# Output projection in order of tokens, and two products of the MLP's first pair set ahead of the last tile's turn

## The chip, the cores and the metric

The kernel runs on one core of a Trainium2 chip. The metric is the device time of one execution in microseconds (us). The trace is of one profiled execution on the chip; all times in it count from the start of its span.

## The reference, cut to what matters

Two layers of a hybrid encoder work on 512 prompt tokens and 256 sample tokens, all in 32-bit floats. What the change touches is the end of the mixer and the start of the MLP:

```python
def encoder_layer(x, ...):
    ...                                     # three branches, gated and summed: merged
    x = x + merged @ w_out                  # output projection, 1024 x 1024
    h2 = rmsnorm(x, norm_ffn)
    u = dwconv(h2 @ ffn_w_up, ffn_conv_w, ffn_conv_b)   # 1024 x 5632
    val, gt = jnp.split(u, 2, axis=-1)
    return x + (jax.nn.silu(gt) * val) @ ffn_w_down
```

## The kernel before

**Tiles and splits.** The 768 tokens are six tiles of 128: tiles 0 to 2 are the first half of the tokens, tiles 3 to 5 the second (`TH` is 384). Each 32-bit operand is split into a high part (an ACT copy to fp32r) and a low part (a DVE subtraction), and each product is three matmuls: high x high, low x high, high x low. Activations are held turned (features on the partitions) in `hTh` and `hTl`.

**The up-projection by pairs.** `pair_products` computes two blocks of 128 features for all tokens by a scheme of seven half-size products instead of eight. With the inputs cut into two halves of the features and two halves of the tokens (`R["11"]`, `R["21"]` for the first half of the tokens, `R["12"]`, `R["22"]` for the second), it needs the sums t1 = 12 - 11, t2 = 22 - t1, t3n = 11 - t2 and t4n = 21 - t2. t1 stands in the place of `R["12"]` in `hTh`/`hTl`; t2, t3n and t4n are the tensors `Eh`/`El`. One product is 12 matmuls of 384 columns.

**What happens to one tile.** In the output projection `t_mm` does 24 matmuls of 512 columns for one tile and one half of the features (line 1265, `wo`); line 1266 adds the result to `x`. In the second half of the features each tile is then normalised (`norm_rows`: a square with sum on ACT, two small operations on POOL, a scaling on DVE, line 427, tile `xn`) and one step later turned (`quad`: eight transposes on TensorE, line 330, tile `tp`). This text calls those transposes the tile's turn.

- A tile of the first half (0 to 2) needs little of DVE afterwards: two low parts (`put`, line 435, `hTl<-tp`). Its turned halves are kept in `qt`.
- A tile of the second half (3 to 5) needs much: t1 (line 461), the low part of 22, t2 (line 464), the low part of t1 (`hTl<-qt`), and then in `e_sums` the low part of t2, two subtractions (lines 469 and 471) and the low parts of t3n and t4n (`El`): nine operations of 128x512.

**The order around the change.** `ORDER` is (0, 3, 1, 4, 2, 5): the tiles of the two halves alternate. The MLP begins with `up(0)`, whose `pair_products` gets `first`: the last tile is turned when `todo[0]()` is evaluated, ahead of the first product X = 11 x w11, and what `quad` returned, `e_sums` of the last tile, runs behind X. The order in which each engine takes its instructions is made by the framework's scheduler, from the order of the code and from its own estimates; `soon` raises an instruction's priority. Each engine works through its own list in order.

**Weights.** `Weights` brings them from memory (`wraw`), splits them on ACT (`whi`, line 206) and DVE (`wlo`, line 207) into six slots, and forms the sums that the pairs need (DVE, lines 217 and 229). A pair takes four slots; the output projection's half takes four too.

Of the kernel before, what the change touches and what calls it, by code (L numbers as in the profile page):

```python
# [9 lines left out]
AF = mybir.ActivationFunctionType  # L10
OP = mybir.AluOpType
# [8 lines left out]
NT = T // P  # L20
# [263 lines left out]
def body(tc, nc, a, depth=DEPTH):  # L284
# [8 lines left out]
    act, tt, stt, ts = (nc.scalar.activation, nc.vector.tensor_tensor,  # L293
                        nc.vector.scalar_tensor_tensor, nc.vector.tensor_scalar)
# [4 lines left out]
    def mxbank(name, tag=None):  # L299

        if tag is None:
            turn[0] ^= 1
            tag = ("mx", "my")[turn[0]]
        return psum.tile([P, 512], F32, name=name, tag=tag, bufs=BANKS[tag])
# [24 lines left out]
    def tr(out, in_):  # L329
# [8 lines left out]
    lo_, hi_ = slice(0, TH), slice(TH, T)  # L338

    R = {"11": [h[:, 0:4, lo_] for h in hT], "21": [h[:, 4:8, lo_] for h in hT],  # L340
         "12": [h[:, 0:4, hi_] for h in hT], "22": [h[:, 4:8, hi_] for h in hT]}
# [28 lines left out]
    def acc_tile():  # L370

        return {0: mxbank("acc", "acc"), TP: mxbank("acc", "acc")}
# [10 lines left out]
    def t_mm(o, t, ws, n, kper):  # L383
        ts_ = slice(t * P, (t + 1) * P)
        for k in range(NK):
            wh, wl = ws[k // kper]
            cs = slice((k % kper) * n, (k % kper) * n + n)
            mm(o, hT[0][:, k, ts_], wh[:, cs], start=(k == 0), stop=False)  # L388
            mm(o, hT[0][:, k, ts_], wl[:, cs], start=False, stop=False)  # L389
            mm(o, hT[1][:, k, ts_], wh[:, cs], start=False, stop=(k == NK - 1))  # L390
# [18 lines left out]
    def st4(name):  # L409
        return base.tile([P, 1024], F32, name=name, tag="st4", bufs=2)  # L410
# [27 lines left out]
    ORDER = (0, 3, 1, 4, 2, 5)  # L438
# [43 lines left out]
    def norm_then(step, t, x, gb, *args):  # L482

        xn = st4("xn")
        norm_rows(xn, x, gb)
        return lambda: step(t, xn, *args)


    def prod(bank, w, r, first):
        for k in range(4):  # L490
            o = bank[:, :TH]
            mm(o, w[0][:, k, :], r[0][:, k, :], start=first and k == 0, stop=False, skip_group_check=True)  # L492
            mm(o, w[0][:, k, :], r[1][:, k, :], start=False, stop=False, skip_group_check=True)  # L493
            mm(o, w[1][:, k, :], r[0][:, k, :], start=False, stop=k == 3, skip_group_check=True)  # L494

    def soon(ins, *args, **kw):
        with tc.high_priority(offset=100):
            ins(*args, **kw)  # L498

    def pair_products(v, g, tmp, done, vtag="acc", pump=0.0, first=None):  # L500

        wa, wb, wd, wc = W.get(4)
        cut = lambda w, o: tuple(x[:, o:o + 512].rearrange("p (k c) -> p k c", c=P) for x in w)
        w = {"11": cut(wa, 0), "22": cut(wa, 512), "12": cut(wd, 0),
             "s2": cut(wb, 0), "s1": cut(wb, 512), "s3": cut(wc, 0), "s4n": cut(wc, 512)}
        p1, u = tmp[:, :TH], tmp[:, TH:T]
        acc = lambda tag="acc": mxbank("acc", tag)[:, :TH]
        X = acc()  # L510
        prod(X, w["11"], R["11"], True)
        soon(act, p1, X, AF.Copy)
        if first:

            first()
            Z = acc()
            prod(Z, w["s1"], R["t1"], True)
            soon(act, g[:, lo_], Z, AF.Copy)
            prod(X, w["12"], R["21"], False)
            soon(act, v[:, lo_], X, AF.Copy)  # L520
            prod(Z, w["s4n"], R["22"], False)
            Y = acc()
            prod(Y, w["s2"], R["t2"], True)
            soon(tt, u, Y, p1, op=OP.subtract)
            soon(stt, v[:, hi_], Z, -1.0, u, op0=OP.mult, op1=OP.subtract)
            V = acc(vtag)
            prod(V, w["22"], R["t4n"], True)
            prod(Y, w["s3"], R["t3n"], False)
            soon(tt, u, Y, p1, op=OP.subtract)
            soon(tt, g[:, hi_], g[:, lo_], u, op=OP.add)  # L530
            soon(tt, g[:, lo_], V, u, op=OP.add)
            W.free(4)
            done(1)
            done(0)
            return
        side.pump(pump)
        pending()
        Y = acc()
        prod(Y, w["s2"], R["t2"], True)
        soon(tt, u, Y, p1, op=OP.subtract)  # L540
        side.pump(pump)
        prod(X, w["12"], R["21"], False)
        soon(act, v[:, lo_], X, AF.Copy)
        W.free()
        side.pump(pump)
        V = acc(vtag)
        prod(V, w["22"], R["t4n"], True)
        W.free()
        side.pump(pump)
        prod(Y, w["s3"], R["t3n"], False)  # L550
        soon(tt, g[:, hi_], Y, p1, op=OP.subtract)
        soon(tt, g[:, lo_], V, g[:, hi_], op=OP.add)
        side.pump(pump)
        Z = acc()
        prod(Z, w["s1"], R["t1"], True)
        soon(tt, g[:, hi_], Z, g[:, hi_], op=OP.add)
        W.free()
        side.pump(pump)
        done(1)

        def rest():
            prod(Z, w["s4n"], R["22"], False)
            soon(stt, v[:, hi_], Z, -1.0, u, op0=OP.mult, op1=OP.subtract)
            W.free()
            side.pump(pump)
            done(0)

        late.append(rest)
# [3 lines left out]
    def pending():  # L572
        while late:
            late.pop(0)()

    def load_gb(i):
        gb = base.tile([P, D], F32, name="gb", tag="gb", bufs=1)
        nc.sync.dma_start(gb, a["norms"][i])
        return gb
# [8 lines left out]
    def layer(l, x_in, prev_x):  # L588
# [559 lines left out]
        def pair(pool, tag, bufs, pump, evac):  # L1148
            vg = [pool.tile([P, T], F32, name=n, tag=tag, bufs=bufs) for n in ("pv", "pg")]
            tmp = pool.tile([P, T], F32, name="pt", tag=tag, bufs=bufs)  # L1150
            pair_products(*vg, tmp, lambda j: evac(j, vg[j]), pump=pump)
# [70 lines left out]
        for b in range(3):  # L1222
# [4 lines left out]
            for mp in range(4):  # L1227
                (wh, wl), = W.get()
                v = lambda w: w[:, :D].rearrange("p (m k c) -> p m k c", m=2, c=P)
                for mi in range(2):  # L1230
# [3 lines left out]
                    acc = acc_tile()  # L1234
# [18 lines left out]
        def ftile(name, tag, bufs=1, dt=F32):  # L1253
            return (ap if tag in ("ah", "al") else fp).tile([P, T], dt, name=name, tag=tag, bufs=bufs)
# [4 lines left out]
        todo = []  # L1259
        for half in range(2):  # L1260
            ws = W.get(4)
            cs = slice(half * 512, half * 512 + 512)
            for t in ORDER:
                ps = mxbank("wo")
                t_mm(ps, t, ws, 512, 2)
                tt(x[:, t, cs], x[:, t, cs], ps, op=OP.add)
                if half == 1:
                    bs = [f() for f in todo]
                    todo = [norm_then(quad, t, x[:, t, :], gb2,
                                      lambda i: ftile("qt", ("ah", "al", "rv", "uv")[i], (4, 4, 1, 1)[i]))]  # L1270
                    for f in bs:
                        f()


        def up(i):

            raw = [ftile("rv", "rv"), ftile("rg", "rg")]
            us = {}
            out = [ftile("ah", "ah", 4, F32R), ftile("al", "al", 4, F32R)]

            def conv(s):
                r, u = raw[s], ftile("u", ("uv", "ug")[s])
                f = i + NFF * s
                w = lambda j: par[:, O_FW + f * 3 + j:O_FW + f * 3 + j + 1]
                act(u, r, AF.Identity, scale=w(1), bias=par[:, O_FB + f:O_FB + f + 1])
                for c0, n in RANGES:
                    stt(u[:, c0 + 1:c0 + n], r[:, c0:c0 + n - 1], w(0), u[:, c0 + 1:c0 + n],
                        op0=OP.mult, op1=OP.add)
                    stt(u[:, c0:c0 + n - 1], r[:, c0 + 1:c0 + n], w(2), u[:, c0:c0 + n - 1],
                        op0=OP.mult, op1=OP.add)  # L1290
                us[s] = u
                if s == 1:
                    act(u, u, AF.Silu)
                    return
                ah, al = out
                tt(u, u, us[1], op=OP.mult)
                act(ah, u, AF.Copy)
                tt(al, u, ah.bitcast(F32), op=OP.subtract)

            pair_products(*raw, st4("pt"), conv, "po", first=todo[0]() if i == 0 else None)  # L1300
            return out

        fin = {}
# [21 lines left out]
        for gi, g in enumerate(DOWN_GROUPS):  # L1325
# [24 lines left out]
            for i, (t, cs) in enumerate(units):  # L1350
# [12 lines left out]
                if end and not last:  # L1363
                    nc.sync.dma_start(x_scr[tsl], x[:, t, :])
                    if i == 1:
                        gbn, todo = load_gb(2 * l + 2), []
# [3 lines left out]
                    todo = [norm_then(spill, t, x[:, t, :], gbn, stage, f_scrs[l + 1], "my")]  # L1370
# [29 lines left out]
```

## Time and profile before

| | |
|---|---|
| time, median of 3 runs | 2605.66 us (2602.86 to 2612.2) |
| the profiled execution's own time | 2605.65 us |
| its span in the trace | 2603.9 us |
| TensorE (PE) busy | 2560.1 us, 98% |
| VectorE (DVE) busy | 1904.2 us, 73% |
| ScalarE (ACT) busy | 1153.4 us, 44% |

Busy is the share of the span in which an engine had an instruction under way; matmuls overlap, so a busy PE is not one at its peak. PE rows are matmuls, PEld rows their weight loads.

### The profile page before, as it was taken

To read this page: it belongs to the slowest core of one execution; us is meant where nothing else is said; L and a number is where in the kernel's file an instruction comes from. 1 tells how busy PE (TensorE), PEld (TensorE's weight loads), DVE (VectorE), ACT (ScalarE), POOL (GpSimd) and SP (SyncE) were. 2 spreads that over 40 slices of the span, in tenths; PEclk is the share of its full clock that TensorE was granted. 3 is DMA by queue.
4 is the path that set the end of the run, shared out by engine and by line. 5 is a ranking of instruction groups with operands and counts; after the bars stand their busy time and mean duration, and the time that the engine had idled before them with its cause. 6 is when DMAs were issued, how large, how long until landed. Compare 5 with 4: busy or idle time off the path is not lost.

```text
span 2603.9 us, 37538 instructions
## 1 busy us (share of the span) xinstructions
PE 2560.1 (98%) x14290; PEld 2353.6 (90%) x14290; DVE 1904.2 (73%) x3204; ACT 1153.4 (44%) x1946; POOL 87.8 (3%) x130
## 2 busy tenths in 40 slices
PE   8999999999999999999999999999999999999998
PEld 8878999999889999999998789999998899999997
DVE  6758876665658887888866688765657598888887
ACT  5434465553235433333454455655432354333343
POOL 0002100000000000000000011100000000000000
PEclk9999999999999999999999999999999999999999
DMA  7356568747522222222453575787474222212222
GB/s 248 108 169 204 190 213 255 223 134 230 158 81 67 67 70 73 65 68 71 135 174 129 163 233 172 219 236 215 132 230 141 73 89 65 62 60 73 74 66 89
DMA packets 168900, 359.65 MB, mean 138 GB/s; under 512 B 16080, under 2 KB 62480, under 8 KB 168720
## 3 DMA queue, kind: packets, MB, share of 16 engines
q1 hardware_dynamic: 168720, 357.25, 43.5%
q8 instruction: 113, 1.85, 0.3%
q14 instruction: 67, 0.55, 0.1%
HBM read 276.87 MB, written 80.31 MB: 137 GB/s over the span
## 4 chain that ended last, share of the span: by engine, by line
PE 85%; DMA 7%; ACT 3%; DVE 3%; issue 1%; SPq 1%; POOL 0%; DVEq 0%; POOLq 0%; ACTq 0%
PE acc L493 12%; PE acc L492 12%; PE acc L494 12%; PE dn L1344 5%; PE dn L1342 5%; PE dn L1343 5%; PE acc L366 4%; PE acc L368 4%; PE acc L367 4%; PE acc L389 3%; PE acc L388 3%; PE acc L390 3%; PE wo L390 2%; PE wo L388 2%; PE wo L389 2%
## 5 line engine op out<-in xcount | busy, mean ns | idle before, releaser
L206 ACT ACTIVATE whi<-wraw 128x1024 fp32r<-128x1024 f32 (+2 forms) x444 | 433.8, 985 | 616.0 <-DMA wraw<-wp 153.3
L207 DVE TENSOR_TENSOR wlo<-wraw,whi 128x1024 fp32r<-128x1024 f32 (+2 forms) x444 | 500.3, 1132 | 189.2 <-ACT whi L206 186.9
L493 PE MATMUL acc<-hTl,whi 128*128 128x384 f32 x1216 | 414.3, 341 | 5.0 <-DVE hTl L435 5.0
L492 PE MATMUL acc<-hTh,whi 128*128 128x384 f32 x1216 | 414.1, 341 | 2.9 <-ACT pt L498 2.0
L494 PE MATMUL acc<-hTh,wlo 128*128 128x384 f32 x1216 | 410.0, 339 | 0.0
L492 PE MATMUL acc<-Eh,whi 128*128 128x384 f32 x912 | 309.3, 340 | 0.9 <-DVE pv L498 0.9
L494 PE MATMUL acc<-Eh,wlo 128*128 128x384 f32 x912 | 307.4, 338 | 0.0
L493 PE MATMUL acc<-El,whi 128*128 128x384 f32 x912 | 306.9, 337 | 0.0
L493 PEld LDWEIGHTS acc<-hTl,whi 128*128 128x128 f32 x1216 | 230.3, 189 | 7.5 <-DVE hTl L435 6.0
L492 PEld LDWEIGHTS acc<-hTh,whi 128*128 128x128 f32 x1216 | 229.9, 189 | 7.4 <-ACT pt L498 3.5
L494 PEld LDWEIGHTS acc<-hTh,wlo 128*128 128x128 f32 x1216 | 229.9, 189 | 0.4
L389 PE MATMUL acc<-wlo,hTh 128*128 128x512 f32 (+1 forms) x576 | 210.1, 366 | 2.6 <-DVE wlo L207 2.6
L388 PE MATMUL acc<-whi,hTh 128*128 128x512 f32 (+1 forms) x576 | 208.8, 364 | 2.9 <-ACT whi L206 2.6
L390 PE MATMUL acc<-whi,hTl 128*128 128x512 f32 (+1 forms) x576 | 209.2, 365 | 0.0
L1343 PE MATMUL dn<-wlo,ah 128*128 128x512 f32 x528 | 207.4, 393 | 0.0
L1344 PE MATMUL dn<-whi,al 128*128 128x512 f32 x528 | 201.8, 394 | 0.0
L1342 PE MATMUL dn<-whi,ah 128*128 128x512 f32 x528 | 200.4, 393 | 0.0
L1357 DVE TENSOR_TENSOR x<-x,dn 128x512 f32<-128x512 f32 x168 | 111.9, 685 | 86.0 <-PE dn L1344 86.0
L366 PE MATMUL acc<-hTh,whi 128*128 128x256 f32 (+1 forms) x512 | 174.0, 340 | 0.0
L492 PEld LDWEIGHTS acc<-Eh,whi 128*128 128x128 f32 x912 | 171.3, 188 | 2.9 <-DVE pv L498 1.9
L368 PE MATMUL acc<-hTh,wlo 128*128 128x256 f32 (+1 forms) x512 | 172.9, 338 | 0.0
L367 PE MATMUL acc<-hTl,whi 128*128 128x256 f32 (+1 forms) x512 | 172.9, 338 | 0.0
(277 smaller groups left out, 4772.3 us busy)
## 6 DMA issues: line engine op xcount, KB each, us to landing
wraw<-wp SPq DMA_DIRECT2D x284, 512.0 KB
g<-gate_scr SPq DMA_DIRECT2D x48, 384.0 KB
cw<-cum_scr SPq DMA_DIRECT2D x48, 256.0 KB
xt<-xbc_scr SPq DMA_DIRECT2D x20, 512.0 KB
bias<-nab SPq DMA_DIRECT2D x40, 256.0 KB
gate_scr<-pg SPq DMA_DIRECT2D x24, 384.0 KB
gate_scr<-pv SPq DMA_DIRECT2D x24, 384.0 KB
ot<-o_scr SPq DMA_DIRECT2D x36, 256.0 KB
```

Source lines behind the costliest of these rows:

```text
L206: self.nc.scalar.activation(hi[:, :n], r, AF.Copy)
L207: self.nc.vector.tensor_tensor(lo[:, :n], r, hi[:, :n].bitcast(F32), op=OP.subtract)
L366: mm(o, wh[:, k, :], rh, start=(k == 0), stop=False)
L388: mm(o, hT[0][:, k, ts_], wh[:, cs], start=(k == 0), stop=False)
L389: mm(o, hT[0][:, k, ts_], wl[:, cs], start=False, stop=False)
L390: mm(o, hT[1][:, k, ts_], wh[:, cs], start=False, stop=(k == NK - 1))
L492: mm(o, w[0][:, k, :], r[0][:, k, :], start=first and k == 0, stop=False, skip_group_check=True)
L493: mm(o, w[0][:, k, :], r[1][:, k, :], start=False, stop=False, skip_group_check=True)
L494: mm(o, w[1][:, k, :], r[0][:, k, :], start=False, stop=k == 3, skip_group_check=True)
L1342: mm(ps, ah[:, tsl], wh[:, cs], start=(j == 0), stop=False)
L1343: mm(ps, ah[:, tsl], wl[:, cs], start=False, stop=False)
L1344: mm(ps, al[:, tsl], wh[:, cs], start=False, stop=(j == n - 1))
```

## The change

The loop over the output projection's tiles goes 0 to 5 instead of alternating (both halves of the features). In the first pair of the MLP the product A = 12 x w21 of the first token half gets a bank of its own and comes right behind X, the two are added by DVE (in place of an accumulation in X's bank and a copy by ACT), and only then is the last tile turned: `todo[0]` is handed over unevaluated and called as `first()()`. The tile for t1 has another tag.

```diff
@@ pair_products
         soon(act, p1, X, AF.Copy)
         if first:
 
-            first()
+            A = acc()
+            prod(A, w["12"], R["21"], True)
+            soon(tt, v[:, lo_], A, p1, op=OP.add)
+            first()()
             Z = acc()
             prod(Z, w["s1"], R["t1"], True)
             soon(act, g[:, lo_], Z, AF.Copy)
-            prod(X, w["12"], R["21"], False)
-            soon(act, v[:, lo_], X, AF.Copy)
             prod(Z, w["s4n"], R["22"], False)
@@ layer
-            for t in ORDER:
+            for t in range(NT):
                 ps = mxbank("wo")
                 t_mm(ps, t, ws, 512, 2)
                 tt(x[:, t, cs], x[:, t, cs], ps, op=OP.add)
                 if half == 1:
                     bs = [f() for f in todo]
                     todo = [norm_then(quad, t, x[:, t, :], gb2,
-                                      lambda i: ftile("qt", ("ah", "al", "rv", "uv")[i], (4, 4, 1, 1)[i]))]
+                                      lambda i: ftile("qt", ("ah", "al", "ug", "uv")[i], (4, 4, 1, 1)[i]))]
@@ up
-            pair_products(*raw, st4("pt"), conv, "po", first=todo[0]() if i == 0 else None)
+            pair_products(*raw, st4("pt"), conv, "po", first=todo[0] if i == 0 else None)
```

**What it moves on TensorE, where the projection ends and the first pair begins.** In the rows `wo` are the projection's matmuls, `tp` a tile's turn, `acc<-hTh` and the like the pair's products; a line of dots stands for the rest of a product. Before, from the end of the last tile's projection (tile 5), with the turn of tile 2, X, the turn of tile 5, and the next product:

```order
L390 MATMUL wo<-whi,hTl 128x512
L330 MATMUL tp<-maskident,xn 128x128 x8
L492 MATMUL acc<-hTh,whi 128x384
L493 MATMUL acc<-hTl,whi 128x384
L494 MATMUL acc<-hTh,wlo 128x384
...
L330 MATMUL tp<-maskident,xn 128x128 x8
L492 MATMUL acc<-hTh,whi 128x384
L493 MATMUL acc<-hTl,whi 128x384
```

After the change, from the end of tile 4's projection: X, the turn of tile 3, the whole projection of tile 5, the turn of tile 4, A, the turn of tile 5, and then a matmul on t1, one on t2 (`Eh`) and the others:

```order
L390 MATMUL wo<-whi,hTl 128x512
L492 MATMUL acc<-hTh,whi 128x384
...
L330 MATMUL tp<-maskident,xn 128x128 x8
L388 MATMUL wo<-whi,hTh 128x512
...
L330 MATMUL tp<-maskident,xn 128x128 x8
L492 MATMUL acc<-hTh,whi 128x384
...
L330 MATMUL tp<-maskident,xn 128x128 x8
L492 MATMUL acc<-hTh,whi 128x384
L492 MATMUL acc<-Eh,whi 128x384
L492 MATMUL acc<-hTh,whi 128x384
```

X has moved from behind tile 5's projection to before it, and between the turn of tile 5 and the first product on t1 no product is left.

**What it moves on VectorE, first place: the adding of tile 4 to `x` and what follows.** `x` is the add behind a projection, `xn` the normalised tile, `qt` the kept or summed halves. Before, up to the weight sum of line 229:

```order
L1266 TENSOR_TENSOR x<-x,wo 128x512
L461 TENSOR_TENSOR qt<-tp,qt 128x512
L435 TENSOR_TENSOR hTl<-tp,hTh 128x4x128
L464 TENSOR_TENSOR qt<-tp,qt 128x512
L427 SCALAR_TENSOR_TENSOR xn<-x,rs,gb 128x1024
L435 TENSOR_TENSOR hTl<-qt,hTh 128x4x128
L207 TENSOR_TENSOR wlo<-wraw,whi 128x512
L469 TENSOR_TENSOR qt<-qt 128x512
L471 TENSOR_TENSOR qt<-qt 128x512
L435 TENSOR_TENSOR El<-qt,Eh 128x4x128
L1266 TENSOR_TENSOR x<-x,wo 128x512
L229 SCALAR_TENSOR_TENSOR wraw<-wraw 128x512
```

Those are tile 2's add, the work on tile 4, and tile 5's add. After the change the same stretch begins with tile 4's add and holds the first work on tile 3:

```order
L1267 TENSOR_TENSOR x<-x,wo 128x512
L461 TENSOR_TENSOR qt<-tp,qt 128x512
L427 SCALAR_TENSOR_TENSOR xn<-x,rs,gb 128x1024
L435 TENSOR_TENSOR hTl<-tp,hTh 128x4x128
L464 TENSOR_TENSOR qt<-tp,qt 128x512
L435 TENSOR_TENSOR hTl<-qt,hTh 128x4x128
L207 TENSOR_TENSOR wlo<-wraw,whi 128x512
L469 TENSOR_TENSOR qt<-qt 128x512
L471 TENSOR_TENSOR qt<-qt 128x512
L435 TENSOR_TENSOR El<-qt,Eh 128x4x128
L229 SCALAR_TENSOR_TENSOR wraw<-wraw 128x512
L1267 TENSOR_TENSOR x<-x,wo 128x512
```

The list is nearly the same row for row, but it is that of the first tile of the second half and not of the second one.

**Second place, up to the low part of tile 5's t1.** Before, from the same weight sum on (two rows of `wlo` are two splits):

```order
L435 TENSOR_TENSOR hTl<-tp,hTh 128x4x128
L435 TENSOR_TENSOR El<-qt,Eh 128x4x128
L435 TENSOR_TENSOR hTl<-tp,hTh 128x4x128
L435 TENSOR_TENSOR El<-qt,Eh 128x4x128
L427 SCALAR_TENSOR_TENSOR xn<-x,rs,gb 128x1024
L207 TENSOR_TENSOR wlo<-wraw,whi 128x1024 x2
L461 TENSOR_TENSOR qt<-tp,qt 128x512
L435 TENSOR_TENSOR hTl<-tp,hTh 128x4x128
L464 TENSOR_TENSOR qt<-tp,qt 128x512
L435 TENSOR_TENSOR hTl<-qt,hTh 128x4x128
```

After the change, between tile 5's add and the rows below, stand an `El`, tile 4's t1, an `El`, tile 4's low part of 22, a weight split of 1024 and tile 4's t2. Then:

```order
L498 TENSOR_TENSOR rv<-acc,pt 128x384
L427 SCALAR_TENSOR_TENSOR xn<-x,rs,gb 128x1024
L435 TENSOR_TENSOR hTl<-qt,hTh 128x4x128
L207 TENSOR_TENSOR wlo<-wraw,whi 128x1024
L469 TENSOR_TENSOR qt<-qt 128x512
L471 TENSOR_TENSOR qt<-qt 128x512
L435 TENSOR_TENSOR El<-qt,Eh 128x4x128
L461 TENSOR_TENSOR qt<-tp,qt 128x512
L217 TENSOR_TENSOR wraw<-wraw 128x512
L435 TENSOR_TENSOR hTl<-tp,hTh 128x4x128
L435 TENSOR_TENSOR El<-qt,Eh 128x4x128 x2
L464 TENSOR_TENSOR qt<-tp,qt 128x512
```

The work on tile 4 now stands between tile 5's add and tile 5's `xn`, and the rest of it between that `xn` and tile 5's t1 and t2; the new addition of A (`rv<-acc,pt`) stands ahead of the `xn`.

## Rows read from the trace of the kernel before

**Rows 1.** From the page: busy time of each engine, its share of the span and its instructions.

```profile
PE 2560.1 (98%) x14290; PEld 2353.6 (90%) x14290; DVE 1904.2 (73%) x3204; ACT 1153.4 (44%) x1946; POOL 87.8 (3%) x130
```

**Rows 2.** The waits of PE from 690 to 1100 us of the span (the output projection and the first third of the MLP in the first layer): who waited for what, us in total, times, the longest.

```profile
PE acc L493 <- DVE hTl L435: 2.5, 2, 1.8
PE acc L492 <- ACT hTh L434: 0.2, 1, 0.2
```

**Rows 3.** The timeline of PE around the end of the projection, first layer: start, duration, instruction; in brackets the idle time before it and what ended it.

```profile
776.04 1.03 PE L330 MATMUL tp<-maskident,xn 128*128 128x128 f32 x8
776.83 0.48 PE L388 MATMUL wo<-whi,hTh 128*128 128x512 f32 x1
...
782.48 1.03 PE L330 MATMUL tp<-maskident,xn 128*128 128x128 f32 x8
783.27 0.48 PE L388 MATMUL wo<-whi,hTh 128*128 128x512 f32 x1
...
788.91 1.04 PE L330 MATMUL tp<-maskident,xn 128*128 128x128 f32 x8
790.20 0.44 PE L492 MATMUL acc<-hTh,whi 128*128 128x384 f32 x1 [0.25 <-ACT hTh L434]
792.46 0.69 PE L493 MATMUL acc<-hTl,whi 128*128 128x384 f32 x1 [1.83 <-DVE hTl L435]
...
795.73 0.34 PE L494 MATMUL acc<-hTh,wlo 128*128 128x384 f32 x1
795.90 1.03 PE L330 MATMUL tp<-maskident,xn 128*128 128x128 f32 x8
...
797.15 0.34 PE L493 MATMUL acc<-hTl,whi 128*128 128x384 f32 x1
...
798.91 0.34 PE L494 MATMUL acc<-hTh,wlo 128*128 128x384 f32 x1
799.08 0.37 PE L492 MATMUL acc<-hTh,whi 128*128 128x384 f32 x1
800.15 0.44 PE L493 MATMUL acc<-hTl,whi 128*128 128x384 f32 x1 [0.69 <-DVE hTl L435]
```

**Rows 4.** Busy time of each engine by stretch: length, then PE, PEld, DVE, ACT and POOL with their instructions, then PE's granted clock (1.00 is full), the DMA share and GB/s. The first line is the four projections from tile 3's turn on to tile 5's end, the others the start of the first pair.

```profile
762.90:788.90 26.00, 26.00 (x131) 21.52 (x130) 18.96 (x28) 13.69 (x25) 2.99 (x8) 1.00 0.00 1
...
793.00:794.00 1.00, 1.00 (x5) 1.00 (x4) 1.00 (x3) 1.00 (x2) 0.61 (x2) 0.50 0.68 184
794.00:795.00 1.00, 1.00 (x5) 1.00 (x4) 1.00 (x2) 0.63 (x2) 0.00 (x0) 0.50 0.75 307
795.00:796.00 1.00, 1.00 (x6) 0.96 (x5) 1.00 (x2) 0.62 (x1) 0.00 (x0) 0.71 0.00 0
796.00:797.00 1.00, 1.00 (x10) 0.83 (x9) 1.00 (x2) 0.84 (x3) 0.00 (x0) 1.00 0.65 111
```

**Rows 5.** The timeline of DVE in the same place.

```profile
774.60 0.69 DVE L435 TENSOR_TENSOR hTl<-qt,hTh 128x512 fp32r<-128x512 f32 x1
775.20 0.69 DVE L469 TENSOR_TENSOR qt<-qt 128x512 f32<-128x512 f32 x1
...
782.68 0.69 DVE L1266 TENSOR_TENSOR x<-x,wo 128x512 f32<-128x512 f32 x1 [1.12 <-PE wo L390]
...
786.32 1.27 DVE L427 SCALAR_TENSOR_TENSOR xn<-x,rs,gb 128x1024 f32<-128x1024 f32 x1
787.52 0.68 DVE L435 TENSOR_TENSOR hTl<-qt,hTh 128x512 fp32r<-128x512 f32 x1
...
790.52 0.68 DVE L1266 TENSOR_TENSOR x<-x,wo 128x512 f32<-128x512 f32 x1
791.12 0.69 DVE L229 SCALAR_TENSOR_TENSOR wraw<-wraw 128x512 f32<-128x512 f32 x1
...
795.32 2.38 DVE L207 TENSOR_TENSOR wlo<-wraw,whi 128x1024 fp32r<-128x1024 f32 x2
797.62 0.68 DVE L461 TENSOR_TENSOR qt<-tp,qt 128x512 f32<-128x512 f32 x1
...
798.81 0.68 DVE L464 TENSOR_TENSOR qt<-tp,qt 128x512 f32<-128x512 f32 x1
799.41 0.68 DVE L435 TENSOR_TENSOR hTl<-qt,hTh 128x512 fp32r<-128x512 f32 x1
801.43 0.69 DVE L217 TENSOR_TENSOR wraw<-wraw 128x512 f32<-128x512 f32 x1 [1.33 <-DMA wraw<-wp]
...
809.93 0.55 DVE L498 TENSOR_TENSOR pt<-acc,pt 128x384 f32<-128x384 f32 x1
```

**Rows 6.** The timeline of ACT in the same place.

```profile
789.55 0.60 ACT L434 ACTIVATE hTh<-tp 128x512 fp32r<-128x512 f32 x1 [2.47 <-PE tp L330]
...
795.38 1.06 ACT L206 ACTIVATE whi<-wraw 128x1024 fp32r<-128x1024 f32 x1 [0.75 <-DMA wraw<-wp]
...
799.53 0.63 ACT L434 ACTIVATE Eh<-qt 128x512 fp32r<-128x512 f32 x1 [0.56 <-DVE qt L464]
800.19 0.49 ACT L498 ACTIVATE rv<-acc 128x384 f32<-128x384 f32 x1
```

**Rows 7.** The timeline of PE at the same place in the second layer.

```profile
2086.05 0.69 PE L493 MATMUL acc<-hTl,whi 128*128 128x384 f32 x1 [1.82 <-DVE hTl L435]
...
2093.73 0.44 PE L493 MATMUL acc<-hTl,whi 128*128 128x384 f32 x1 [0.69 <-DVE hTl L435]
```

## The prediction

> **What bounds the kernel now.** The table of busy time says where to begin: PE is busy for 98% of the span, no other engine for more than 73% [rows 1]. So the time changes by what PE gains or loses, and by nothing else as long as that holds. The second view is the waits of PE in the stretch that the change touches. From 690 to 1100 us PE waits three times, 2.7 us in all, for low or high parts that DVE and ACT make of turned tiles [rows 2]; in the rest of the MLP's first third it never waits. The third view, PE's timeline, shows the three waits in their place [rows 3]: X's first matmul waits 0.25 us for tile 2's high part, its second 1.83 us for the low part, and the product on t1 0.69 us for the low part of tile 5's t1. The reader is to see one thing more there: the turn of tile 5 at 795.90 follows X without a gap. The normalising of the last tile, which the change wants to cover, is not what PE waits for.
>
> Whom PE waits for is in the stretches and in DVE's timeline. During the four projections from 762.9 to 788.9 DVE is busy for 18.96 of 26.0 us; from 793 to 797 it is busy for every microsecond [rows 4]. Its list then runs without idle time from tile 4's work to the low part of tile 5's t1 at 799.41 [rows 5], and PE goes on 0.05 us after that has ended, at 800.15 [rows 3]. So the end of this passage is set by DVE's list and not by PE. The second layer shows the same at 2086.05 and 2093.73, with the same waits [rows 7].
>
> **What the change does to PE.** X needs tiles 0 to 2 alone. In token order these are turned after the projection of tile 3, and the scheduler sets X between tile 4's projection and tile 3's turn. The wait of X goes: its low parts are two projections old. In the times of the kernel before: tile 4's projection starts at 776.83 and ends at 782.48 [rows 3], X follows with 12 matmuls of 0.176 us (797.15 to 798.91 is ten of them), 2.1 us, and tile 3's turn starts at 784.6 instead of a turn at 782.48. The projection of tile 5 then ends at 784.6 + 0.8 (turn, 782.48 to 783.27) + 5.65 = 791.0, tile 4's turn at 791.8, A at 793.9. X, A and six turns are the same work as before; only the waits can differ.
>
> **What it does to DVE, step by step.** The nine operations that a tile of the second half needs stood under projections for two of the three tiles. Now the light tiles come first, when DVE has time to spare, and all three heavy ones behind tile 3's turn.
>
> - DVE has added tile 4 to `x` by 783.3 (782.68 + 0.6) and must wait for tile 3's turn. The first four transposes reach another engine 0.64 us after a turn's start (788.91 to 789.55 [rows 3, 6]); tile 3's t1 thus starts at 785.2. DVE idles for 1.9 us there.
> - From tile 3's t1 to tile 5's t2 the changed list holds 25 operations of 512 columns, two `xn`, two splits of 1024 and the new addition. One of 512 takes 0.60 us of the list (774.60 to 775.20), an `xn` 1.20 (786.32 to 787.52), a split of 1024 1.15 (795.32 to 797.62 for two), the addition 0.55 at most, taken from the same form behind the first pair [rows 5]. The last operation, t2, starts after 24 x 0.60 + 2 x 1.20 + 2 x 1.15 + 0.55 = 19.65 us, at 804.85, and ends 0.68 later, at 805.5.
> - ACT then makes the high part (0.04 us on, 0.63 long [rows 5, 6]) and PE takes it 0.05 later: 806.25. That is the `Eh` row behind the first matmul on t1, and nothing can pass it.
>
> Before, PE stood at the same count of products (X, A and one matmul) at 800.15. The difference is **6.1 us** in each layer. A second way to the same size: a heavy tile's nine operations against a light tile's two are 7 x 0.60 = 4.2 us that moved behind the point where DVE had slack, and 1.9 us that it now idles.
>
> What else stands in that list hides. Tile 5's `xn` is done only at 798.4 (15 operations of 0.60, an `xn`, a split and the addition after 785.2 give 797.1, and 1.28 for itself), so PE idles from 793.9 to 798.4 before the turn, but it would have waited for t2 anyway. The addition of A comes up at 796.6, later than A's end, and so waits for nothing; the copy that it replaces took 0.49 us on ACT [rows 6], which has time. Two weight transfers could hold up the list. One starts when line 229 has read its buffer (791.8 before, 791.9 now) and was there 3.5 us later, at 795.38 [rows 5, 6]; its split comes up at 798.9. The other was there at 801.43, 4.9 us after the first of the two splits ended (796.5) [rows 5]; now that split ends at about 796.0 and the sum of line 217 comes up at 802.4, with 1.5 us to spare. SP's list differs by one weight transfer that changes place with its neighbour, POOL's not at all. X, A and Z have the three banks of their kind, and Y gets X's, copied out long before.
>
> **The clock.** Behind the wait of 1.83 us PE's granted clock is 0.50 from 793 to 795 and back at full by 796 [rows 4]: the lower of its two levels, 1.2 GHz instead of 2.4. X's matmuls from the second to the twelfth took 3.27 us there (792.46 to 795.73) and 1.76 at full clock [rows 3]: 1.5 us lost, which cost nothing before, since DVE's list set the end. In the changed kernel PE idles for about 11 us between 793.9 and 806.25, with a turn and one matmul in it. I expect one such stretch behind it, and there PE has its inputs and is the bound again: **1.5 us** per layer, with bounds of 0 (the clock is back by then) and 3.0 (twice the stretch).
>
> The Trainium skill ("TensorE: Matmul & The Clock Gate", What's actually happening) holds that in modelling the ramp of the clock is below one per cent of a usual kernel's span and shouldn't be fitted. By that the sum would have the 6.1 us alone.
>
> **The sum.** The profiled execution's own time is 2605.65 us, the median of the runs 2605.66, so no correction is due. 2 x (6.1 + 1.5) = 15.2 us: 2620.9, said as **2621 us**, 0.6% slower. About 0.5% (13 us, so from 2618.7) is what a measurement of this kernel can tell from no change.
>
> The rest of the MLP is taken at nothing: PE has no wait between 802 and 1100 [rows 2]. But DVE comes out of the passage with its list behind, so one weight split (1.23 us, half of the 2.38 [rows 5]) may come late in the second pair; 0 to 1.2 us per layer, of which I take 0. The first half of the features is only reordered, and no PE wait stands there to move.
>
> **The rivals.**
>
> 1. *The clock costs nothing or the list is shorter than laid out.* If the stretch at 1.2 GHz lies under the wait, as it did before, 2 x 6.1 = 12.2 us are left: 2617.9, within 0.5%. For it speaks that before the slow stretch was covered; against it that the slow stretch reached 3 us into the work behind the wait [rows 4], and that here nothing behind the wait is late enough to cover it.
> 2. *It does what it says, and is not slower.* The waits of X and of t1 go (0.25 + 1.83 + 0.69 = 2.8 us per layer) with X's slow stretch (1.5): at most 8.6 us in two layers, 2597. It decides if tile 5's t2 is ready by 800.2, that is, if DVE gets through the list 6.1 us sooner than its rows say, by a pace of 0.36 us instead of 0.60. Every row of that form stands at 0.60 or above; against the case also that the list is taken in order. Since all that PE loses here is 8.6 us, below 13, faster by over 0.5% is nearly excluded.
> 3. *The backlog goes on.* A transfer comes later than the 1.5 us to spare, or the second pair waits for a split (1.2) and falls to the lower clock again (1.5): with all of it 2 x (6.1 + 3.0 + 1.2 + 1.5) = 23.6, so 2626 to 2630.
>
> **How the numbers follow.** The forecast as laid out (2616 to 2625) gets 0.66, rival 1 with times below that (2611 to 2616, and the middle ground) 0.14, rival 2 0.07, rival 3 0.13. The range of 2612 to 2629 leaves out rival 2, the lower edge of 1 and the upper end of 3, less than 2 in 10. Slower by over 0.5% is the forecast's part above 2618.7 (0.56) and rival 3: 0.69. Within 0.5% are the rest of the forecast, rival 1 and rival 2 but for 0.02: 0.29. Faster: 0.02.
>
> **What would show it.** In the changed kernel's timeline X runs at full clock without a wait before tile 3's turn; PE waits three times behind A, for `xn`, for the high part of tile 5's t1 and for `Eh`; DVE is without a gap from tile 3's t1 to tile 5's t2, 20.3 us long; and the granted clock is 0.5 for some 3 us after the `Eh` row. The forecast is wrong if that row comes less than 14 us after tile 5's projection has ended (806.25 - 791.0 = 15.25), or if PE's waits in the rest of the MLP differ from those of before by more than 2 us.

## The result and the profile after

The changed kernel takes 2624.47 us (median of 6 runs, 2620.07 to 2626.82) against 2605.16 us of the kernel before beside it: a ratio of 1.0077 with a 95% interval of 1.0065 to 1.0090, slower by 0.8%. The page of the changed kernel answers to [rows 1]:

```profile
PE 2566.4 (98%) x14290; PEld 2356.1 (90%) x14290; DVE 1906.0 (73%) x3206; ACT 1150.9 (44%) x1944; POOL 86.7 (3%) x130
```

The instructions are as many as before, and no engine is busy for more than 7 us longer. The span is 2623.9 us instead of 2603.9, so the question is where PE stood still or ran slowly. The waits of PE from 690 to 1100 us, which answer to [rows 2]:

```profile
PE tp L330 <- DVE xn L427: 4.3, 1, 4.3
PE acc L492 <- ACT hTh L434: 2.8, 1, 2.8
PE acc L492 <- ACT Eh L434: 2.3, 1, 2.3
PE acc L492 <- DVE rg L498: 0.3, 1, 0.3
```

In place of 2.7 us there are 9.7. PE's timeline shows where, and answers to [rows 3]:

```profile
784.29 0.34 PE L492 MATMUL acc<-hTh,whi 128*128 128x384 f32 x1
...
786.23 0.34 PE L494 MATMUL acc<-hTh,wlo 128*128 128x384 f32 x1
786.40 1.04 PE L330 MATMUL tp<-maskident,xn 128*128 128x128 f32 x8
792.82 1.03 PE L330 MATMUL tp<-maskident,xn 128*128 128x128 f32 x8
...
795.62 0.33 PE L494 MATMUL acc<-hTh,wlo 128*128 128x384 f32 x1
800.26 1.94 PE L330 MATMUL tp<-maskident,xn 128*128 128x128 f32 x8 [4.31 <-DVE xn L427]
804.98 0.69 PE L492 MATMUL acc<-hTh,whi 128*128 128x384 f32 x1 [2.77 <-ACT hTh L434]
807.98 0.69 PE L492 MATMUL acc<-Eh,whi 128*128 128x384 f32 x1 [2.32 <-ACT Eh L434]
...
813.52 0.33 PE L494 MATMUL acc<-hTh,wlo 128*128 128x384 f32 x1
```

X runs at full clock and without a wait ahead of tile 3's turn (784.29 to 786.40), A follows tile 4's turn; then PE waits three times up to the `Eh` row at 807.98. From there 17 steps to 813.52 take 5.54 us, 0.33 each instead of 0.176. The stretches say why (columns as in [rows 4]):

```profile
800.00:804.00 4.00, 1.94 (x8) 1.57 (x8) 4.00 (x7) 1.63 (x3) 0.00 (x0) 0.50 0.62 209
...
812.00:813.00 1.00, 1.00 (x5) 1.00 (x5) 1.00 (x2) 0.45 (x1) 0.00 (x0) 0.50 0.00 0
813.00:814.00 1.00, 1.00 (x6) 1.00 (x5) 0.96 (x3) 0.04 (x1) 0.00 (x0) 0.79 0.00 0
814.00:815.00 1.00, 1.00 (x8) 1.00 (x7) 0.55 (x1) 0.04 (x1) 0.00 (x0) 1.00 0.00 0
```

The granted clock is at half, the lower of the two levels, from 800 us (the end of the first wait) until past 813 us, and up to 813 us DVE is busy throughout. DVE's timeline, which answers to [rows 5]:

```profile
784.49 0.69 DVE L1267 TENSOR_TENSOR x<-x,wo 128x512 f32<-128x512 f32 x1 [1.96 <-PE wo L390]
787.04 0.69 DVE L461 TENSOR_TENSOR qt<-tp,qt 128x512 f32<-128x512 f32 x1 [1.86 <-PE tp L330]
...
798.85 1.27 DVE L427 SCALAR_TENSOR_TENSOR xn<-x,rs,gb 128x1024 f32<-128x1024 f32 x1
...
803.58 0.68 DVE L461 TENSOR_TENSOR qt<-tp,qt 128x512 f32<-128x512 f32 x1
...
806.59 0.68 DVE L464 TENSOR_TENSOR qt<-tp,qt 128x512 f32<-128x512 f32 x1
```

It idles 1.86 us for tile 3's turn, and then there is no gap from tile 3's t1 (787.04) to the end of tile 5's t2 (807.27). The second layer repeats it (PE; compare [rows 7]):

```profile
2102.28 1.94 PE L330 MATMUL tp<-maskident,xn 128*128 128x128 f32 x8 [4.29 <-DVE xn L427]
2107.00 0.69 PE L492 MATMUL acc<-hTh,whi 128*128 128x384 f32 x1 [2.77 <-ACT hTh L434]
2110.00 0.69 PE L492 MATMUL acc<-Eh,whi 128*128 128x384 f32 x1 [2.32 <-ACT Eh L434]
```

**How the profiles are compared.** The lists of all engines up to the changed place are the same instruction for instruction in the first layer, and yet tile 0's turn starts at 764.93 us after the change and at 763.23 before; of these 1.70 us 1.66 already stand at the projection's first matmul (724.57 against 722.91). So all distances below count from the start of tile 0's turn in each layer: to the *resume row* (the matmul behind the last of the waits) and to the last matmul of the layer's MLP. The first is 43.05 us in layer 1 (807.98 - 764.93) and 42.98 in layer 2, before 36.92 and 37.05.

| kernel | resume row, layers 1 and 2, us | last matmul of the MLP, us | ratio of times to before |
|---|---|---|---|
| before | 36.92, 37.05 | 540.02, 539.35 | |
| before, a second profile | 36.93, 37.15 | 540.05, 539.46 | |
| after | 43.05, 42.98 | 550.03, 549.02 | 1.0077 (1.0065 to 1.0090) |
| order_alone | 42.79, 42.72 | 549.08, 547.67 | 1.0063 (1.0050 to 1.0076) |
| pair_alone | 37.54, 40.47 | 542.75, 544.91 | 1.0026 (1.0017 to 1.0035) |
| less | 40.99, 40.91 | 547.69, 546.21 | 1.0059 (1.0047 to 1.0072) |
| warm | 43.05, 42.96 | 547.17, 546.47 | 1.0056 (1.0044 to 1.0068) |
| sums_last | 39.01, 38.91 | 544.92, 545.00 | 1.0048 (1.0035 to 1.0061) |
| pool | 44.62, 44.69 | 550.30, 549.43 | 1.0088 (1.0074 to 1.0102) |
| pool_before | 38.75, 39.61 | 541.87, 541.93 | 1.0017 (1.0006 to 1.0027) |
| tile4_sums_late | 35.22, 35.15 | 539.85, 539.55 | 1.0003 (0.9994 to 1.0013) |

### The profile page after: what moved, and what is told of

It is laid out like the page before. It is cut to its first block, busy times and chain, and to the rows that moved or that the text cites. A ratio compares the mean times of both kernels' runs of the same rounds, so it can differ in the third digit from the quotient of the medians.

```text
span 2623.9 us, 37559 instructions
## 1 busy us (share of the span) xinstructions
PE 2566.4 (98%) x14290; PEld 2356.1 (90%) x14290; DVE 1906.0 (73%) x3206; ACT 1150.9 (44%) x1944; POOL 86.7 (3%) x130
## 4 chain that ended last, share of the span: by engine, by line
PE 81%; DMA 7%; DVE 6%; ACT 3%; issue 2%; SPq 1%; POOL 0%; DVEq 0%; POOLq 0%; ACTq 0%
PE acc L492 12%; PE acc L493 12%; PE acc L494 12%; PE dn L1345 5%; PE dn L1343 5%; PE dn L1344 5%; PE acc L368 4%; PE acc L366 4%; PE acc L367 4%; PE acc L389 3%; PE acc L388 3%; PE acc L390 3%; DMA cw<-cum_scr 2%; PE wo L388 2%; PE wo L390 2%
## 5 line engine op out<-in xcount | busy, mean ns | idle before, releaser
L494 PEld LDWEIGHTS acc<-Eh,wlo 128*128 128x128 f32 x912 | 171.2, 188 | 1.0
```

## The experiments

**A second profile of the kernel before** (no edit).

> The kernel before, unchanged, in one more profile. It tells what a difference between two profiles is worth. If the start of tile 0's turn (763.23 us in the shown profile, 764.5 to 769.4 in the changed kernels, whose lists are the same up to there) moves by some us from execution to execution, that part of a difference of spans is none of the change's. The distances from tile 0's turn to the row behind the waits (36.92 and 37.05 us) and to the last matmul of the MLP (540.0 and 539.35 us) should come back within 0.3 us; if the second one moves by 1 us, the 1 us a layer that I can't place in the changed kernel is none either.

Tile 0's turn starts at 764.08 instead of 763.23, and at 2053.17 instead of 2056.68 in layer 2: differences of spans of a few us carry no meaning. The distances come back within 0.11 us, so differences in them of 0.3 us do. One thing more came of it. In layer 2 the clock stayed at full behind the wait of 1.82 us this time (the last row, columns as in [rows 4]; before it was at 0.50 from 2086 to 2089), X ended earlier, and PE waited for DVE and ACT instead:

```profile
2082.54 0.44 PE L493 MATMUL acc<-hTl,whi 128*128 128x384 f32 x1 [1.82 <-DVE hTl L435]
2085.63 1.07 PE L330 MATMUL tp<-maskident,xn 128*128 128x128 f32 x8 [0.89 <-DVE xn L427]
2087.05 0.44 PE L492 MATMUL acc<-hTh,whi 128*128 128x384 f32 x1 [0.35 <-ACT pt L498]
2090.32 0.45 PE L493 MATMUL acc<-hTl,whi 128*128 128x384 f32 x1 [0.69 <-DVE hTl L435]
...
2082.00:2084.00 2.00, 1.46 (x8) 1.46 (x9) 2.00 (x4) 2.00 (x4) 0.81 (x2) 1.00 0.36 86
```

The resume row is at 37.15 us, against 37.05 in the profile of [rows 7]. This shows what the prediction had only argued: X's slow stretch in the kernel before cost nothing.

**Which half of the change.** The order alone:

```diff
-            for t in ORDER:
+            for t in range(NT):
                 ps = mxbank("wo")
```

> The kernel before with the output projection in order of tokens, and nothing else (the first pair keeps X, the last tile's turn, the product on t1, and A at the end of X's accumulation). Measure: the distance from the start of tile 0's turn to the first matmul that runs without a stop on the sums of tile 5 (the row after which PE has no wait: before 800.15 - 763.23 = 36.9 us in layer 1 and 2093.73 - 2056.68 = 37.05 in layer 2; after 807.98 - 764.93 = 43.05 and 42.98). My theory (the order puts three heavy tiles on DVE behind tile 3's turn, and DVE's list sets the end): nearly the whole loss comes from this part alone, 42.4 to 43.1 us, a slow stretch of 2 to 3 us behind it, 16 to 20 us in the time, a ratio to before of 1.006 to 1.0077. Rival 1 (the pair's part is what costs: the last tile's turn waits behind A and its xn is the longest wait, 4.3 us): less than half of it, 37 to 40 us, ratio 1.000 to 1.003. Rival 2 (both are needed): in between.

The pair's part alone (after, with `for t in ORDER` put back):

> The changed kernel with the projection's order of before (0, 3, 1, 4, 2, 5): only the pair's part of the change, A in a bank of its own ahead of tile 5's turn, added by DVE. My theory (order is the cause): DVE has done tiles 3 and 4 under the projections as before; its list is longer by the new addition alone (0.5 us), but tile 5's turn now stands behind A, 2.1 us later on PE, so that t1 comes some 0.5 to 2.5 us later; 37.4 to 39.5 us on the measure of the run with the order alone, ratio 1.000 to 1.004 with a slow stretch of up to 2.5 us. Rival 1 (this part is the cause): 41 us or more, ratio 1.005 or more. Rival 3 (the part does what it says, covering the last tile's normalising): below 36.5 us, ratio 0.997 to 0.999.

The order alone gives 5.9 and 5.7 us of the 6.1 and 5.9 at the resume row and 1.0063 of 1.0077. PE's timeline in layer 1 follows. A comes ahead of the turn of tile 5 here too, since the scheduler set it there without the pair's part of the change; it still shares X's bank:

```profile
796.62 0.69 PE L492 MATMUL acc<-hTh,whi 128*128 128x384 f32 x1 [3.05 <-ACT pt L498]
...
800.62 1.91 PE L330 MATMUL tp<-maskident,xn 128*128 128x128 f32 x8
...
807.41 0.69 PE L492 MATMUL acc<-Eh,whi 128*128 128x384 f32 x1 [2.21 <-ACT Eh L434]
```

A waits 3.05 us for X's copy, starts 32.0 us behind tile 0's turn instead of 28.7 as in the changed kernel, and runs at half clock. The `Eh` row comes 0.26 us earlier even so (42.79 against 43.05): when A runs on PE doesn't matter to it. So the two kernels can't say what moving A ahead of the turn is worth, since both have it there.

The pair's part alone costs 0.6 us at the resume row in layer 1, about the length of the new addition (0.55 us), which stands ahead of tile 5's t1. In layer 2 it costs 3.4 (40.47 us, where I had allowed for 39.5):

```profile
2094.63 0.68 DVE L461 TENSOR_TENSOR qt<-tp,qt 128x512 f32<-128x512 f32 x1
2096.94 0.69 DVE L217 TENSOR_TENSOR wraw<-wraw 128x512 f32<-128x512 f32 x1 [1.64 <-DMA wraw<-wp]
2097.55 0.68 DVE L435 TENSOR_TENSOR hTl<-tp,hTh 128x512 fp32r<-128x512 f32 x1
```

There the weight sum of line 217 stands between tile 5's t1 and its low part, and DVE waits 1.64 us for the transfer, with 0.60 for the sum itself: the mishap with weight transfers that the prediction looked for in the changed kernel, where it did not happen. The order is the cause of most of the loss (0.63% and 0.26% apart, 0.77% together, with intervals of about 0.1% each). What the pair's part adds to the order, 0.14%, is hardly clear of these intervals.

**Does the length of DVE's list set the row?** Four operations fewer on DVE; the low parts that they make are zeros, so this kernel leaves out a part of the products:

```diff
+    def thin(name, c, src):
+        hi, lo = (r[:, :, c * P:(c + 1) * P] for r in R[name])
+        act(hi, src, AF.Copy)
+        act(lo, src, AF.Copy, scale=0.0)
...
-        put("t4n", c, f21)
+        (thin if mlp and c < 2 else put)("t4n", c, f21)
-        put("t3n", c, f11)
+        (thin if mlp and c < 2 else put)("t3n", c, f11)
```

> The changed kernel with four operations fewer on DVE in each layer: the low parts of t3n and t4n of tiles 3 and 4 (four of the nine-operation lists' last parts, 128x512 each) are written as zeros by ACT, which has time; so the computation is not the reference's there. My theory (the end of the passage is set by the length of DVE's list at 0.60 us an operation): the row behind which PE runs without a stop comes 4 x 0.60 = 2.4 us earlier, 40.6 us after tile 0's turn instead of 43.0; the waits of PE sink by that sum; the slow stretch behind stays; ratio to before 1.0077 - 2 x 2.4/2605 = 1.0059. Rival (the chain of the last tile sets it: projection, add, square, POOL's two operations, xn, turn, t1): no DVE operation off that chain matters, 42.8 to 43.1 us, ratio 1.0077.

The row comes 2.06 and 2.07 us earlier where 2.4 was expected; the last matmul 2.3 and 2.8. Of the missing 0.3, 0.25 has a row: DVE's list now has a gap ahead of tile 5's `xn`, and it is POOL that ends it.

```profile
798.30 0.55 DVE L503 TENSOR_TENSOR rv<-acc,pt 128x384 f32<-128x384 f32 x1
799.09 1.29 DVE L427 SCALAR_TENSOR_TENSOR xn<-x,rs,gb 128x1024 f32<-128x1024 f32 x1 [0.25 <-POOL rs L419]
```

So the list sets the row, and the chain of the last tile (add, square, POOL, `xn`) is close behind it.

**The list reordered, nothing left out.** `e_sums` of tiles 3 and 4 are queued on DVE behind tile 5's t2 (`first()` turns tile 5 and returns `e_sums` of tiles 5, 3 and 4):

```diff
-        tt(t2, ps[1], t1, op=OP.subtract)
+        last["low"] = tt(t2, ps[1], t1, op=OP.subtract)
...
-            first()()
+            fs = first()
+            with tc.issue_after(last["low"].ins):
+                for f in fs:
+                    f()
```

> The changed kernel with e_sums of tiles 3 and 4 (five DVE operations each: the low part of t2, two subtractions, two low parts) queued on DVE behind tile 5's t2; the t2 of tiles 3 and 4 get the spare buffers of `ah` and `al`. Nothing is left out. My theory (the list's length up to tile 5's t2 sets the Eh row, and DVE's whole work up to the end of the first pair sets a second bound): ten operations or 6.0 us leave the list ahead of t2. DVE then has gaps again and the chain of the last tile takes over: its projection ends 27.9 us after tile 0's turn, then add 0.7, square 1.2, POOL about 1.2, xn 1.3, half a turn 0.6, t1 0.7, t2 0.7 or more, high part 0.6; so the Eh row at 37 to 39.5 us instead of 43.0. Then PE overtakes DVE: a new wait of 1 to 3 us for a low part (t2, t4n or t3n) within the next 8 us, since the ten operations are still to be done. Net 2 to 4 us a layer, ratio 1.0045 to 1.0065. Rival (only t2's place matters, the sums afterwards are hidden): no new wait, 4 to 6 us a layer, ratio 1.003 to 1.0045.

The row is at 39.01 and 38.91 us, 4.0 us earlier and within what was expected; tile 5's `xn` (793.47) now waits 0.72 us for POOL, as the chain of the last tile would have it. The second half of my expectation fell: PE's waits name none in the 8 us behind the row (layer 2 has two short ones, 0.2 and 0.3 us, some 390 us later), and the last matmul is 5.1 and 4.0 us earlier. The ten operations set back were hidden behind PE's work. The rival was right in this, by the rows; the ratio of 1.0048 lies in the range of my expectation and just above the rival's, and its interval covers parts of both; that PE ran at half clock behind the row and so left DVE time may be part of why, but wasn't tried. The kernel is still slower than the one before.

**The clock by itself.** Matmuls into a spare bank fill PE's waits:

```diff
+    def idle(bank, w, r, n, ins):
+        for j in range(n):
+            with tc.issue_after(ins.ins):
+                ins = mm(bank[:, :TH], w[0][:, j % 4, :], r[0][:, j % 4, :], start=True, stop=True)
+        return ins
...
-            first()()
+            spare = mxbank("spare", vtag)
+            ins = idle(spare, w["12"], R["21"], 24, ins)
+            with tc.issue_after(ins.ins):
+                sums = first()
+            ins = idle(spare, w["12"], R["21"], 36, last["tr"])
+            sums()
```

> The changed kernel with 24 added matmuls of 128x384 behind A and 36 behind tile 5's turn, into a spare bank that nothing reads: 24 x 0.176 = 4.2 and 36 x 0.176 = 6.3 us of work for PE inside its waits of 4.3, 2.8 and 2.3 us and the turn that ran at half clock. Everything else stays in its order. My theory: DVE's list sets when the Eh row can start, so it still comes 43.0 us after tile 0's turn (42.6 to 43.3), but PE's clock is at full there, and the 17 matmuls behind it that took 5.54 us in layer 1 take 17 x 0.176 = 3.0: 2.5 us less in each layer, ratio 1.0077 - 5/2605 = 1.0058. Rival (the slow stretch costs nothing, since the pair behind it waits for DVE anyway, as the wait for rg of 0.3 and 0.9 us shows): the clock is full, the gain turns into waits for DVE behind, ratio 1.0070 to 1.0077. If the added matmuls delay the turn, the row comes later than 43.5 us and the run says nothing of the clock.

```profile
800.24 4.37 PE L502 MATMUL spare<-hTh,whi 128*128 128x384 f32 x24
804.72 1.06 PE L332 MATMUL tp<-maskident,xn 128*128 128x128 f32 x8
805.54 6.58 PE L502 MATMUL spare<-hTh,whi 128*128 128x384 f32 x36
811.96 0.33 PE L494 MATMUL acc<-hTh,whi 128*128 128x384 f32 x1
812.43 0.44 PE L494 MATMUL acc<-Eh,whi 128*128 128x384 f32 x1
...
800.00:816.00 16.00, 15.76 (x92) 15.15 (x91) 16.00 (x25) 9.04 (x15) 1.63 (x2) 1.00 0.28 92
```

Tile 0's turn is at 769.38 here, so the `Eh` row stands at 43.05 us, to 0.01 us where it stood: 60 matmuls more on PE, and not one counts, since DVE sets the row. The granted clock is 1.00 throughout (last row), the 17 steps behind the row take 3.08 us instead of 5.54 (the 12 slow ones of layer 2 take 2.22 instead of 3.96), and the last matmul comes 2.9 and 2.6 us earlier. The wait for `rg` at 838 us (0.3, and 0.9 in layer 2) is gone too. So the slow clock costs 5.4 us in two layers: 4.2 in the slow steps themselves, none of it hidden, and 1.2 in the waits for `rg` that go with it (why they go isn't shown).

**Off DVE, onto POOL.** Four subtractions of each layer:

```diff
-        tt(f21, f21, t2, op=OP.subtract)
+        eng = nc.gpsimd.tensor_tensor if mlp and c < 2 else tt
+        eng(f21, f21, t2, op=OP.subtract)
-        tt(f11, f11, t2, op=OP.subtract)
+        eng(f11, f11, t2, op=OP.subtract)
```

> The changed kernel with four subtractions of each layer (f21 - t2 and f11 - t2 of tiles 3 and 4, 128x512, all operands in SBUF) on POOL instead of DVE. My theory of the list: 4 x 0.60 = 2.4 us off it, the Eh row 40.6 us after tile 0's turn, ratio 1.0059, provided that POOL does one in under about 2.4 us and doesn't slow DVE. No row of before shows such an operation on POOL; its nearest rows are 128x1. Rival: POOL and DVE get in each other's way, rows of DVE of 0.68 become longer while POOL works; with one of DVE's operations held up for each of POOL's, nothing is gained or it is lost: Eh row 42.5 to 46 us, ratio 1.0075 to 1.010.

> The kernel before with the same four subtractions of tiles 3 and 4 on POOL in each layer. In the kernel before DVE's list is full from 793 us on; tile 3's two subtractions lie where DVE has time, tile 4's two (1.2 us) in the full part. By the theory of the list PE's waits of 1.83 and 0.69 us shrink by up to 1.2 us in all: 0 to 1.2 us a layer, ratio 0.999 to 1.000. If POOL and DVE get in each other's way, 0.5 to 4 us a layer are lost: ratio 1.0005 to 1.003.

The rival's outcome, twice: the resume row comes 1.6 and 1.7 us later than in the changed kernel (the time, 1.0088, can't be told from its 1.0077), and 1.8 and 2.6 us later than in the kernel before (1.0017). POOL's rows and then DVE's in the changed kernel with this edit:

```profile
791.67 1.68 POOL L470 TENSOR_TENSOR qt<-qt 128x512 f32<-128x512 f32 x1 [2.88 <-DVE qt L464]
793.32 1.73 POOL L472 TENSOR_TENSOR qt<-qt 128x512 f32<-128x512 f32 x1
```

```profile
791.51 0.68 DVE L435 TENSOR_TENSOR hTl<-qt,hTh 128x512 fp32r<-128x512 f32 x1
792.11 1.80 DVE L207 TENSOR_TENSOR wlo<-wraw,whi 128x512 fp32r<-128x512 f32 x1
793.83 1.76 DVE L435 TENSOR_TENSOR El<-qt,Eh 128x512 fp32r<-128x512 f32 x1
795.51 0.68 DVE L229 SCALAR_TENSOR_TENSOR wraw<-wraw 128x512 f32<-128x512 f32 x1
```

While POOL works, an operation of 0.68 us on DVE takes 1.76 to 1.80: 1.1 us lost for each 0.6 saved. The expectation was wrong in one point: the kernel before does have operations of 128x512 on POOL (twelve products, line 851), and there DVE's rows do not get longer (see the last section).

**A try at beating both.** The kernel before, with `e_sums` of tile 4 alone queued behind the low part of tile 5's t1:

```diff
-        put("t1", c, t1)
+        last["low"] = put("t1", c, t1)
...
-            first()
+            with tc.issue_after(last["low"].ins):
+                for f in first:
+                    f()
```

> The kernel before, its order and its pair, with one thing moved: e_sums of tile 4 (five DVE operations, 3.0 us) is queued on DVE behind the low part of tile 5's t1; tile 4's t2 gets a spare buffer of `al`. Nothing is left out. By the theory of DVE's list: the low part of tile 2 that X waits for (1.83 us) and that of tile 5's t1 (0.69 us) come earlier, X stays at full clock, and the row behind the waits comes 1 to 2.5 us earlier than before's 36.9 to 37.05 us after tile 0's turn; what tile 5's projection and normalising take (its add, square, POOL, xn) is the next bound. As in the run with the sums of tiles 3 and 4 set back, I expect no large new wait behind, at most 0.5 us. Net 0.7 to 2 us a layer, 538 to 539.3 us from tile 0's turn to the last matmul of the MLP instead of 540.0, ratio 0.9985 to 0.9995. Rival (DVE's whole work up to the end of the pair is the bound, and what is gained is given back): 539.8 to 541 us, ratio 0.9995 to 1.001.

```profile
794.10 0.44 PE L493 MATMUL acc<-hTl,whi 128*128 128x384 f32 x1 [0.42 <-DVE hTl L435]
796.77 1.06 PE L330 MATMUL tp<-maskident,xn 128*128 128x128 f32 x8 [0.48 <-DVE xn L427]
798.59 0.45 PE L492 MATMUL acc<-hTh,whi 128*128 128x384 f32 x1 [0.75 <-ACT pt L498]
801.35 0.44 PE L493 MATMUL acc<-hTl,whi 128*128 128x384 f32 x1 [0.21 <-DVE hTl L435]
```

The wait of 1.83 us becomes 0.42, and the resume row is 1.7 and 1.9 us earlier (801.35 - 766.13 = 35.22). At the last matmul 0.2 us earlier in layer 1 and 0.2 later in layer 2 is left of it. About 0.5 us of the give-back has a row in each layer, a wait for a weight's low part later in the MLP; where the rest went isn't settled. So my expectation of a gain fell and its rival, that what is gained is given back, came: 1.0003 is no gain, and no kernel here beats the one before.

## Why the prediction was right

**What bounds the passage** was right: DVE's list and not PE. The run with added matmuls (PE busy, row unmoved) and that with four operations fewer on DVE (row 2.1 us earlier) show it from both sides.

**The 6.1 us.** The distance from tile 0's turn to the resume row grew by 6.13 and 5.93 us. In the changed kernel's trace all rows stand 1.7 to 1.8 us later than laid out, of which 1.7 is the drift from before the changed place: X at 784.29 (782.48 laid out), tile 3's t1 at 787.04 (785.2), `xn` at 798.85 (797.1), t2 at 806.59 (804.85), the `Eh` row at 807.98 (806.25). The gapless list is 20.23 us long (20.3). Summing a list by row durations was good to 0.1 us, because the list has no gap.

**The clock: right in kind, too small.** I had 1.5 us per layer, taken from the slow part of X in the kernel before, which follows a wait of 1.83 us. Behind 9.4 us of waits the slow stretch cost 5.54 - 17 x 0.1755 = 2.6 us in layer 1, and 3.96 - 12 x 0.1755 = 1.9 in layer 2 (0.1755 is a step at full clock), within the bounds of 0 to 3.0. By the run with added matmuls it is 5.4 us in two layers instead of 3.0, with the 1.2 of the waits for `rg` that go with it. The sentence of the Trainium skill that the prediction weighed ("TensorE: Matmul & The Clock Gate", What's actually happening), that the ramp is below one per cent of a usual span, holds in its number: 5.4 of 2624 us is 0.2%. But it is over a quarter of what this change costs, and without it the forecast would have been 2617.9.

**The rest of the MLP: taken at 0, and wrong in the term.** Layer 1's last matmul came 10.0 us later and layer 2's 9.7, 19.7 in all. Less 12.06 at the resume rows and 5.4 for the clock, 2.2 us are left, 1.0 and 1.2, at the upper end of the bounds of 0 to 1.2. It is not the wait that I named: PE waits for no weight split there. What it waits for is `rg`, which DVE adds, 0.3 and 0.9 us; the run with the order alone has no such wait, and with the clock at full it is gone from its place. In layer 1 of that kernel one step of 0.48 us (at 906.82, for `rg` again) is all that stands out, 0.3 us longer than its neighbours, and the rest is spread: single steps of the pair's matmuls average 0.1753 us without it (0.1750 before, in both profiles), and those of the down projection 0.2315 (0.2312), 0.8 us over some 2540 steps. What slows them isn't settled.

**The sum.** 15.2 predicted; 12.1 + 5.4 + 2.2 = 19.7 by the distances, 19.3 by the medians. It was 4.5 us too small by the distances, for the clock (2.4) and the rest of the MLP (2.2), two misses on the same side, so that nothing cancelled; the forecast of 2621 is 3.5 us too low by the time. The time lies inside the range of 2612 to 2629 and on the side, slower by over 0.5%, that had 0.69. The two signs that would have made it wrong did not come: the row is over 15 us behind tile 5's projection (807.98 - 792.82), and the waits of PE in the rest of the MLP are 0.3 and 0.9 us. Rival 1 is out by the run with full clock; rival 2 by the row's place; rival 3's transfer was not late here, and its 23.6 us were not reached.

## What to carry to other kernels

When an engine off the critical path has a saturated list, look at which work stands under cover and which behind it: a reorder that puts the light items first and the heavy ones last moves work out of its cover, and PE pays for it even though each wait that the change aims at does go away. Ask of any wait of PE of several us what the clock is behind it, and whether anything late there covers the slow steps. A gain at one row (1.7 us here) is no gain until the end of the stretch has been looked at.

## What the runs showed of the hardware

- POOL (GpSimd) and DVE stood in each other's way. With subtractions on POOL (two runs) one of 128x512 took 1.27 to 2.29 us there, and a DVE operation of that size with two inputs in SBUF that began under it 1.75 to 1.80 instead of 0.68. The Trainium skill ("SBUF — State Buffer", Who interferes with whom) says that a DVE instruction with two SBUF inputs contends with a GpSimd instruction that reads SBUF; the rows agree. Which of the two loses is not always the same: in the kernel before, a product of 128x512 on POOL takes 1.04 to 6.18 us, while 35 of the 36 two-input subtractions, additions and products of 128x512 that DVE does under these keep 0.69 to 0.71. What decides it isn't shown.

```profile
278.89 6.18 POOL L851 TENSOR_TENSOR y<-xs,par 128x512 f32<-128x512 f32 x1 [18.14 <-DVE y L863]
279.25 0.70 DVE L471 TENSOR_TENSOR fq<-fq 128x512 f32<-128x512 f32 x1
```

- The lower clock does not follow each wait of the same length: behind 1.82 us of waiting it came in one profile of the kernel before, at the same matmul, and not in the other.
- How far the program has come at a given row differs by some us between executions with identical lists up to there (tile 0's turn at 761.5 to 769.4 us in layer 1, those with POOL included); distances within a passage repeat to 0.1 us.
